# A two-layer hybrid encoder step on one core: an earlier rotary table, a longer sleep in the bf16 row norms, and sample loads that wait for the previous batch's pages

## The chip, the cores and the metric

The kernel runs on one core of one Trainium2 chip. The metric is the device time of one execution in microseconds, lower is better. Its instructions run on five engines: TensorE (PE, matmuls and transposes), VectorE (DVE), ScalarE (ACT), GpSimd (POOL) and SyncE (SP, which here issues most DMAs). Each engine works through its own queue in order.

## The reference, cut to what matters

Two layers run over the same 1168 columns: 16 meta tokens, 1024 prompt frames and 8 sample streams of 16 frames each. A layer has three parallel groups of heads (latent attention, mLSTM, gated DeltaNet), whose gated outputs are mixed back into the stream:

```python
proj = rms_norm(x, norm_w) @ w_in
(c_q, c_kv, k_r, z_a, m_q, m_k, m_v, m_i, m_f, m_o, z_m, g_qkv, g_a, g_b, z_g) = split(proj)
q = rms_norm(c_q, q_norm) @ w_uq          # 8 heads, 64 plain and 32 rotary columns each
q_rope = apply_rope(q[..., 64:], pos)
c_new = rms_norm(c_kv, kv_norm)           # the latent rows, 256 wide
o_a = mla_attention(...)                  # prompt: plain; samples: absorbed, over 1056 cached latent rows each
...
mixed = concat([o_a * silu(z_a), o_m * silu(z_m), o_g * silu(z_g)])
x = x + mixed @ w_out
```

For the samples, the attention of each of the 8 batches reads its own cached latent rows (1040 x 256) twice: transposed for the scores, and by rows for the product of probabilities and rows.

## The kernel before, in words

The order of the instructions is made while the kernel is built, by a small planner (`Weave`). It keeps a clock `W.t` that each matmul (`mm`) and transpose (`tr`) advances by a cost written into the code, and a list of threads (generators). A thread that yields a number sleeps that many microseconds of the planner's clock; one that yields a key waits until the key is in `D1`. While no thread is due, the planner takes the next piece of the filler `main()`: in each layer the projections `projs` (24 matmuls for each output tile and slice of columns, with split weights so that fp32r and bf16 products together give fp32), then the attention projections `qkv`, `out_first` and `out_proj`. So a sleep is a number of PE matmuls of the filler that are put between two pieces of a thread. The framework then orders the other engines' queues by the same dependences.

Large tiles are pages: 28 (`NPG`) of 128 x 1200 floats. `pg()` takes one, `free()` gives it back, and `room(n)` says whether n are left. A thread that needs pages asks `room` and sleeps for a number of its own until it is answered with yes.

The change touches three places.

`rstd` (L480 to L517) makes the scale of a row norm: column sums of squares by matmuls against a column of ones, then on DVE and POOL the power -0.5 (L495, L496), a split of the result into two parts (L499, L500), diagonals with the scale on them (L506, L508), a sleep, and two matmuls of those diagonals against a matrix of ones (`onesr`) that broadcast the scale. With `b16` the column sums take bf16 parts. `prep` is the only caller with `b16`: two norms (the latent rows `ckv`, the query latents `cq`) in each of three column slices, in each layer.

`prep` (L1347 to L1382) then scales and splits the latents, stores the new latent rows, transposes the sample columns of them (L1375), copies and stores these to `tok` and frees `ckv`. `qkv` (L1387 on) starts when `prep` is done and 10 pages are free. It takes two pages for the rotary table `tabq`, loads them, and multiplies the rotary query tiles (j = 0 and 3) by them (L1420, L1423, added on POOL at L1425). The rotary rows go to `qS` in HBM and come back to be split (L1530, L1531); between them lie the k and v projections (L1458 to L1483).

The samples run as six threads over 8 batches. `samp_load` takes three pages of raw rows for a batch (two of `latT`, one of `krT`), as long as fewer than 5 (`RP`) are in flight and 5 pages (1 + `SR`) are free; it asks every 0.3 us. `samp_split` splits them (L1698 to L1702), `samp_s` makes the scores and exponentials (L1753). `samp_ln` takes two pages for the rows `latN` of a batch, when 4 pages (2 + `SP`) are free; it asks every 8.8 us and, from batch 2 on, waits first for the end (`su`) of the batch two before. `samp_t` transposes the probabilities and multiplies them with `latN`; its last copies are at L1796.

Of the kernel before, what the change touches and what calls it, by code (L numbers as in the profile page):

```python
# [19 lines left out]
T = 1168  # L20
# [8 lines left out]
SR = 4  # L29
SP = 2  # L30
RP = 5
# [276 lines left out]
def _build(nc, tc, ctx, I, O, layers):  # L308
# [13 lines left out]
    def nm(p):  # L322
        uid[0] += 1
        return f"{p}{uid[0]}"

    def pg(dt=F32):
        n = nm("pg")
        t = pgp.tile([128, 2 * PG if dt == BF16 else PG], dt, tag="pg", name=n)
        pages[id(t)] = t
        if len(pages) > NPG:  # L330
            raise RuntimeError("out of pages")
        return t

    def free(*ts):
        for t in ts:
            del pages[id(t)]

    def room(n):
        return len(pages) + n <= NPG

    def need(n):
        while not room(n):
            yield 0.09
# [7 lines left out]
    def pb():  # L351
        return pbp.tile([128, 512], F32, tag="pb", name=nm("pb"))
# [4 lines left out]
    def wt(tag, w=128, bufs=2, dt=F32):  # L357
        return wk.tile([128, w], dt, tag=tag, name=nm("wk"), bufs=bufs)

    def mm(out, lhsT, rhs, start, stop):  # L360
        W.last = P.matmul(out, lhsT, rhs, start=start, stop=stop)  # L361
        n = rhs.free_size()
        if rhs.dtype == BF16:
            W.t += max(n / 2.4, 35.0)
        elif rhs.dtype != F32:
            W.t += max(n / 2.4, 107.0)
        else:
            m = lhsT.free_size()
            W.t += max(n / 0.6, 216.0) if m > 64 else max(n / 0.6, 124.0) if m > 32 else 85.0 if lhsT.partition_size() > 32 else 40.0
# [8 lines left out]
    def gate(inst):  # L378
        if W.last is not None:
            tc.add_manual_dep(inst.ins, W.last.ins.name, NOSYNC, reason="order of slots")  # L380

    def ld(dst, src, eng=None):
        gate((eng or nc.sync).dma_start(dst, src))

    def st(dst, src):
        nc.sync.dma_start(dst, src)
# [34 lines left out]
    def negh(w):  # L421
        return neg1.to_broadcast([128, w])
# [4 lines left out]
    def vcol(l, n, j):  # L427
        o = (l * VW + VEC[n][0]) if l < L else 2 * VW
        return vec[:, o + j:o + j + 1]
# [35 lines left out]
    def sumsq(pgs, w, s0, s1):  # L465
        acc = wt("hp", 528, 3)
        for k, p_ in enumerate(pgs):
            if k == 0:
                S.activation(acc[:, :w], p_[:, s0:s1], AF.Square)
            else:  # L470
                b = wt("th", 400)
                S.activation(b[:, :w], p_[:, s0:s1], AF.Square)
                V.tensor_add(acc[:, :w], acc[:, :w], b[:, :w])
        return acc[:, :w]

    def rstd(out, a, dim, s0, s1, b16=False):
        w = s1 - s0
        tl = [c for c in range(NT) if s0 <= OFF[c] < s1]
        ps = pb()
        col = wt("col", 8)  # L480
        V.memset(col, 1.0)
        if b16:
            ab = wt("th", 800, 2, BF16)
            ah, al = ab[:, :w], ab[:, 400:400 + w]
            S.copy(ah, a)
            V.tensor_sub(al, a, ah)
        for j, c in enumerate(tl):
            n, o = LEN[c], OFF[c] - s0
            if b16:
                mm(ps[:n, j:j + 1], ah[:, o:o + n], onesb, True, False)  # L490
                mm(ps[:n, j:j + 1], al[:, o:o + n], onesb, False, True)
            else:
                mm(ps[:n, j:j + 1], a[:, o:o + n], ones[:, 0:1], True, True)
        for j0, j1, n in (((0, 1, 16), (1, len(tl), 128)) if tl[0] == 0 else ((0, len(tl), 128),)):
            V.tensor_scalar(col[:n, j0:j1], ps[:n, j0:j1], 1.0 / dim, EPS, op0=ALU.mult, op1=ALU.add)  # L495
        G.tensor_tensor(col[:, 0:len(tl)], col[:, 0:len(tl)], negh(len(tl)), op=ALU.pow)  # L496
        nt = len(tl)
        ch = wt("ch", 8, 2, F32R)
        V.tensor_copy(ch[:, 0:nt], col[:, 0:nt])  # L499
        V.tensor_sub(col[:, 0:nt], col[:, 0:nt], ch[:, 0:nt].bitcast(F32))  # L500
        dg = wt("dg", 1024, 1, F32R)
        first = 16 if tl[0] == 0 else 0
        for e, c_ in enumerate((ch, col)):
            o = 512 * e
            if first:
                V.tensor_scalar_mul(dg[:, o:o + 16], ident[:, 0:16], c_.bitcast(F32)[:, 0:1])  # L506
            m = nt - (first > 0)
            V.tensor_tensor(dg[:, o + first:o + w].rearrange("p (j t) -> p j t", t=128),  # L508
                            ident.unsqueeze(1).to_broadcast([128, m, 128]),
                            c_.bitcast(F32)[:, nt - m:nt].unsqueeze(2).to_broadcast([128, m, 128]), op=ALU.mult)  # L510
        yield 2.70
        ps = pb()
        for e in range(2):
            mm(ps[:, :w], onesr, dg[:, 512 * e:512 * e + w], e == 0, e == 1)
        if out is None:
            return ps[:, :w]
        S.copy(out, ps[:, :w])  # L517

    def norm_split(p_, rp, wcol, hi, lo, s0, s1):
        V.scalar_tensor_tensor(p_[:, s0:s1], p_[:, s0:s1], wcol, rp, op0=ALU.mult, op1=ALU.mult)  # L520
        split(p_[:, s0:s1], hi[:, s0:s1], lo[:, s0:s1])
# [65 lines left out]
    def layer(l, XH, XLp, XL, xres, xw, R):  # L587
# [3 lines left out]
        D1 = W.done = {}  # L591
# [751 lines left out]
        def prep():  # L1343
            yield ("cq", 2)
            yield from need(2)
            cq = [D1["cq", j] for j in range(3)]
            ckv = [D1["ckv", j] for j in range(2)]  # L1347
            r1, r2 = pg(), pg()
            for s0, s1 in SLICES:
                w = s1 - s0  # L1350
                yield from rstd(r1[:, s0:s1], sumsq(ckv, w, s0, s1), 256.0, s0, s1, True)
                yield from rstd(r2[:, s0:s1], sumsq(cq, w, s0, s1), 384.0, s0, s1, True)
            while not room(4):
                yield 3.47
            yield 5.44
            hl = {}
            for n_, p_, r_, v_ in (("ck", ckv, r1, "kvn"), ("cq", cq, r2, "qn")):
                hl[n_] = []
                for k, t_ in enumerate(p_):
                    yield from need(2)  # L1360
                    hi, lo = pg(F32R), pg(F32R)
                    for s0, s1 in SLICES:
                        norm_split(t_, r_[:, s0:s1], vcol(l, v_, k), hi, lo, s0, s1)
                        yield 6.23
                    hl[n_].append((hi, lo))
                    if n_ == "cq":
                        free(t_)
                free(r_)
                if n_ == "ck":
                    for k in range(2):  # L1370
                        st(O["oLat"][l, k], ckv[k][:, :T])
                        G.tensor_copy(new[:, 128 * k:128 * k + 128], ckv[k][:, TP:T])
                    ps = pb()
                    for k in range(2):
                        tr(ps[:, 128 * k:128 * k + 128], ckv[k][:, TP:T], ident)  # L1375
                    t_ = wt("hp", 528, 3)
                    S.copy(t_[:, 0:256], ps[:, 0:256])
                    st(tokS, t_[:, 0:256])
                    free(*ckv)
                A.update({n_ + "h": [x_[0] for x_ in hl[n_]], n_ + "l": [x_[1] for x_ in hl[n_]]})  # L1380
            D1["prep"] = 1

        KS = ((0, 348), (348, 694), (694, 1040))

        def qkv():
            while "prep" not in D1 or not room(10):
                yield "idle"  # L1387
            tab, qs = [pg(), pg()], pg()
            A["qs"] = qs
            for j in range(2):  # L1390
                ld(tab[j][:, :T], I["tabq"][j])
            ckh, ckl, cqh, cql = A["ckh"], A["ckl"], A["cqh"], A["cql"]

            def load(t_):
# [272 lines left out]
        def samp_load():  # L1667
            yield "sprep"
            fly = A["fly"] = []
            for b in range(8):  # L1670
                for k in range(3):
                    while len(fly) >= RP or not room(1 + SR):
                        yield 0.30
                    raw = pg()
                    fly.append(raw)
                    p_, src = (slice(0, 128), I["latT"][l, b, :, k]) if k < 2 else (slice(0, 96), I["krT"][l, b])
                    ld(raw[p_, :TP], src)
                    G.tensor_copy(raw[p_, TP:NK], new[p_, 128 * k + 16 * b:128 * k + 16 * b + 16])
                    D1["raw", b, k] = raw, W.t / 1000.0 + YL
                    yield 0.00  # L1680
# [290 lines left out]
        A = {}  # L1971
# [20 lines left out]
```

## Time and profile before

| | |
|---|---|
| median of 3 runs | 2650.75 us (2647.45 to 2651.11) |
| the profiled execution | 2646.51 us, its span 2644.6 us |
| mean granted clock of PE | 0.978 |
| PE busy | 2488.7 us (94%) |
| PE weight loads | 2150.1 us (81%) |
| DVE, ACT, POOL busy | 58%, 42%, 29% |
| DMA | 97 GB/s over the span |

The profile is of one execution. A row of its timeline gives the start and length of an instruction, its engine and source line, what it writes and reads, and in brackets how long the engine stood idle before it and what ended that (idle time followed by "<-" and the instruction or DMA that came last). The granted clock is the share of full speed that PE was given in a stretch.

### The profile page before, as it was taken

The page shows a single profiled execution, that of the slowest core. Times are in us where ns is not written, and L with a number is a line of the kernel's source. Part 1 is how long each engine was busy: PE and PEld are TensorE (multiplying, and loading weights), DVE is VectorE, ACT ScalarE, POOL GpSimd, SP SyncE. Part 2 cuts the span into 40 slices and gives each one's busy share as a digit, 9 for nine tenths or more (in the row PEclk, how much of TensorE's full clock was granted, in tenths as well). Part 3 has the DMA queues.
Part 4 walks back from the last instruction along what each step waited for, and adds up shares of the span by engine and source line. Part 5 has one row for each costly group of instructions (what it writes and reads, how often), then busy time and mean ns, then how long its engine had stood idle before and what let it go on. Part 6 is the DMA issues. An engine that isn't in the chain of part 4 may idle for free. (4 is left out here: it accounts for less than half of the span.)

```text
span 2644.6 us, 45521 instructions
## 1 busy us (share of the span) xinstructions
PE 2488.7 (94%) x17310; PEld 2150.1 (81%) x17310; DVE 1530.2 (58%) x3716; ACT 1116.4 (42%) x2635; POOL 764.6 (29%) x865
## 2 busy tenths in 40 slices
PE   6999999999999899979998999999999999999997
PEld 4887888878878789779977888788788788897896
DVE  6667475464453476654566774755743526665636
ACT  5363444444433433442343544444444434334612
POOL 3122222122123543232441222221221245332414
PEclk9999999999999999989998999999999999998998
DMA  3212112121123644464422121221211245444832
GB/s 130 73 39 70 51 53 83 51 69 51 59 71 126 179 119 123 126 219 163 141 76 51 43 75 52 62 73 51 69 52 58 85 157 149 113 121 147 286 117 80
DMA packets 158411, 258.67 MB, mean 98 GB/s; under 512 B 48704, under 2 KB 110768, under 8 KB 158192
## 3 DMA queue, kind: packets, MB, share of 16 engines
q1 hardware_dynamic: 152224, 247.59, 30.0%
q0 software_dynamic: 1856, 3.86, 0.7%
q10 hardware_dynamic: 4112, 4.30, 0.7%
q8 instruction: 137, 2.24, 0.3%
q14 instruction: 82, 0.67, 0.1%
HBM read 190.77 MB, written 64.92 MB: 97 GB/s over the span
## 5 line engine op out<-in xcount | busy, mean ns | idle before, releaser
L361 PE MATMUL pa<-pg,wh 128*128 128x384 f32 (+3 forms) x6324 | 1317.8, 351 | 17.7 <-DVE pg L441 7.0
L361 PEld LDWEIGHTS pa<-pg,wh 128*128 128x128 f32 x6324 | 1104.6, 190 | 59.9 <-issue 8.5
L361 PE MATMUL pb<-pg,pg 128*128 128x352 f32 (+26 forms) x1908 | 425.1, 338 | 18.3 <-DVE sm L1553 4.4
L361 PE MATMUL pa<-pg,wb 128*128 128x384 bf16 (+1 forms) x2208 | 420.3, 330 | 4.7 <-POOL pg L544 3.6
L361 PEld LDWEIGHTS pb<-pg,pg 128*128 128x128 f32 (+7 forms) x1908 | 301.1, 188 | 70.8 <-issue 14.0
L361 PEld LDWEIGHTS <-wb 128*128 128x128 bf16 x2208 | 201.6, 98 | 141.6 <-issue 28.9
L361 PE MATMUL pb<-wk,pg 128*128 128x128 f32 (+4 forms) x2168 | 223.1, 250 | 20.2 <-ACT wk L983 5.2
L441 POOL TENSOR_TENSOR wh<-wf,wh 128x1024 fp32r<-128x1024 f32 (+1 forms) x61 | 144.4, 2367 | 323.1 <-ACT wh L437 316.7
L361 PEld LDWEIGHTS pb<-wk,pg 128*128 128x128 f32 (+3 forms) x2168 | 194.2, 161 | 41.9 <-issue 16.7
L1590 ACT ACTIVATE wk<-pb 128x320 f32<-128x320 f32 (+8 forms) x288 | 114.1, 407 | 241.9 <-PE pb L361 222.5
L361 PE MATMUL pa<-wk,pg 128*128 128x320 f32 (+8 forms) x576 | 190.9, 417 | 1.9 <-ACT wk L1590 1.3
L437 ACT CAST wh<-wf 128x1024 fp32r<-128x1024 f32 (+1 forms) x122 | 126.4, 1036 | 129.8 <-PE pa L361 119.5
L1553 DVE TENSOR_REDUCE sm<-pb 128x1 f32<-128x348 f32 (+9 forms) x232 | 107.9, 493 | 102.4 <-PE pb L361 89.9
L1613 DVE RECIPROCAL wk<-pa 64x320 f32<-64x320 f32 (+2 forms) x48 | 110.7, 2305 | 48.2 <-PE pa L361 47.5
L361 PE MATMUL pb<-wk,wk 32*32 32x16 f32 (+6 forms) x1776 | 110.6, 216 | 13.7 <-DVE wk L1131 4.5
L1531 POOL TENSOR_TENSOR pg<-pg,pg 64x520 fp32r<-64x520 f32 (+1 forms) x64 | 86.9, 1369 | 111.0 <-ACT pg L1530 87.9
L868 DVE SCALAR_TENSOR_TENSOR pg<-pg,vec,pg 128x1192 f32<-128x1192 f32 x72 | 107.1, 1503 | 18.4 <-ACT pg L866 18.1
L441 DVE TENSOR_TENSOR wh<-wf,wh 128x1024 fp32r<-128x1024 f32 (+1 forms) x61 | 78.6, 1289 | 53.5 <-ACT wh L437 53.4
L693 ACT COPY pg<-pa 128x384 f32<-128x384 f32 (+1 forms) x108 | 52.1, 482 | 134.6 <-PE pa L361 133.4
L457 ACT CAST wb<-wf 128x1024 bf16<-128x1024 f32 x92 | 96.2, 1045 | 26.6 <-PE pa L361 20.1
L361 PEld LDWEIGHTS pa<-wk,pg 128*128 128x128 f32 (+1 forms) x576 | 97.9, 193 | 5.9 <-ACT wk L1590 1.9
L361 PEld LDWEIGHTS pb<-wk,wk 32*32 32x32 f32 (+2 forms) x1776 | 73.1, 122 | 32.3 <-issue 9.3
(298 smaller groups left out, 3205.7 us busy)
## 6 DMA issues: line engine op xcount, KB each, us to landing
wf<-win SPq DMA_DIRECT2D x92, 512.0 KB
pg<-latT SPq DMA_DIRECT2D x32, 520.0 KB
pg<-latN SPq DMA_DIRECT2D x32, 512.0 KB
wf<-wout SPq DMA_DIRECT2D x24, 512.0 KB
xa<-wk SPq DMA_DIRECT2D x40, 192.0 KB
mix<-pg SPq DMA_DIRECT2D x12, 584.0 KB
pg<-mix SPq DMA_DIRECT2D x12, 584.0 KB
mix<-pg SPq DMA_DIRECT2D x12, 576.0 KB
```

The source lines that it names most:

```text
L361: W.last = P.matmul(out, lhsT, rhs, start=start, stop=stop)
L437: S.copy(hi, src)
L441: lo_eng.tensor_sub(lo, src, hi.bitcast(F32))
L457: S.copy(wb[:, :n], wf)
L693: S.copy(o[:, s0:s1], ps)
L868: V.scalar_tensor_tensor(y[:, :n], cb[:, j:j + n], vcol(l, "cw", 4 * ti + j), y[:, :n], op0=ALU.mult, op1=ALU.add)
L1531: G.tensor_sub(lo, raw, hi.bitcast(F32))
L1553: V.tensor_reduce(mx[:LEN[c], 3 * c + i_:3 * c + i_ + 1], ps[:LEN[c], :n1 - x_], axis=AX.X, op=ALU.min)
L1590: S.activation(pt[:m, :b - a], ps, AF.Exp, scale=-1.0)
L1613: V.reciprocal(rc, po[d, :w])
```

## The change

One sleep in `rstd` becomes longer where the row norm has bf16 parts. The two pages and loads of the rotary table move from the start of `qkv` into `prep`, right behind the store of the transposed sample columns and the freeing of `ckv`; `qkv` takes them over and asks for 8 free pages instead of 10. And `samp_load` doesn't take a page for batch b > 0 before `samp_ln` has taken batch b-1's.

```diff
--- before.py
+++ after.py
@@ -508,7 +508,7 @@
-        yield 2.70
+        yield 4.00 if b16 else 2.70
         ps = pb()
@@ -1377,18 +1377,19 @@
                     S.copy(t_[:, 0:256], ps[:, 0:256])
                     st(tokS, t_[:, 0:256])
                     free(*ckv)
+                    A["tab"] = [pg(), pg()]
+                    for j in range(2):
+                        ld(A["tab"][j][:, :T], I["tabq"][j])
...
         def qkv():
-            while "prep" not in D1 or not room(10):
+            while "prep" not in D1 or not room(8):
                 yield "idle"
-            tab, qs = [pg(), pg()], pg()
+            tab, qs = A["tab"], pg()
             A["qs"] = qs
-            for j in range(2):
-                ld(tab[j][:, :T], I["tabq"][j])
             ckh, ckl, cqh, cql = A["ckh"], A["ckl"], A["cqh"], A["cql"]
@@ -1669,7 +1670,7 @@
                 for k in range(3):
-                    while len(fly) >= RP or not room(1 + SR):
+                    while len(fly) >= RP or not room(1 + SR) or b and ("ln", b - 1) not in D1:
                         yield 0.30
                     raw = pg()
```

## Rows read from the trace of the kernel before

**Rows 1.** The page's busy times: engine, us, share of the span, instructions.
```profile
PE 2488.7 (94%) x17310; PEld 2150.1 (81%) x17310; DVE 1530.2 (58%) x3716; ACT 1116.4 (42%) x2635; POOL 764.6 (29%) x865
```

**Rows 2.** PE's waits, 750:790, then 2060:2096: us in total, times, longest.
```profile
PE pb L361 <- DVE wk L508: 5.1, 6, 2.3
...
PE pb L361 <- DVE wk L508: 4.2, 5, 1.5
```

**Rows 3.** Timeline of the first row norm: start, length, engine, line, operation.
```profile
753.15 2.39 POOL L441 TENSOR_TENSOR wh<-wf,wh 128x1024 fp32r<-128x1024 f32 x1
753.22 2.34 DVE L499 CAST wk<-wk 128x4 fp32r<-128x4 f32 x1 [1.13 <-POOL wk L496]
...
756.51 0.42 PE L361 MATMUL pb<-wk,onesr 128*128 128x400 f32 x1 [1.29 <-DVE wk L508]
```

**Rows 4.** Timeline of SP's queue around the table loads of layer 0.
```profile
830.10 0.33 SPq L386 DMA_DIRECT2D tok<-wk  x1
830.48 0.70 SPq L383 DMA_DIRECT2D pg<-tabq  x1
841.30 0.32 SPq L386 DMA_DIRECT2D mix<-pg  x1
841.73 0.37 SPq L383 DMA_DIRECT2D pg<-tabq  x1
```

**Rows 5.** Timelines of DVE, POOL, ACT and PE behind the table, layer 1 last.
```profile
845.45 0.57 DVE L1420 SCALAR_TENSOR_TENSOR pg<-pa,pg 128x400 f32<-128x400 f32 x1 [3.09 <-PE pa L361]
847.10 1.16 DVE L1423 SCALAR_TENSOR_TENSOR wk<-pa,pg 64x400 f32<-64x400 f32 x2 [1.08 <-DMA pg<-tabq]
...
851.04 2.40 POOL L441 TENSOR_TENSOR wh<-wf,wh 128x1024 fp32r<-128x1024 f32 x1
853.39 1.01 POOL L1425 TENSOR_TENSOR pg<-pg,wk 128x384 f32<-128x384 f32 x1
...
864.75 0.62 ACT L1530 CAST pg<-pg 96x520 fp32r<-96x520 f32 x1 [5.37 <-DMA pg<-qS]
...
865.77 6.46 PE L361 MATMUL pa<-wh,pg 128*128 128x512 f32 x21 [3.60 <-ACT pg L1459]
...
2173.78 6.55 PE L361 MATMUL pa<-wh,pg 128*128 128x512 f32 x16 [4.45 <-ACT pg L1459]
```

**Rows 6.** SP's queue in the sample stage: two rows of layer 0, one of layer 1.
```profile
1091.83 0.89 SPq L383 DMA_DIRECT2D pg<-latT  x2
...
1142.14 0.89 SPq L383 DMA_DIRECT2D pg<-latN  x2
...
2432.94 1.05 SPq L383 DMA_DIRECT2D pg<-latN  x2
```

**Rows 7.** PE's waits in 1130:1172, then in 2430:2475: us in total, times, longest.
```profile
PE pa L372 <- ACT pg L1753: 7.2, 3, 4.1
PE pb L361 <- DMA pg<-latN: 4.1, 1, 4.1
...
PE pb L361 <- ACT pg L1753: 2.3, 1, 2.3
```

**Rows 8.** Windows: us, busy (instructions) of PE, PEld, DVE, ACT, POOL, clock, DMA.
```profile
1130.00:1170.00 40.00, 26.13 (x150) 23.78 (x149) 22.21 (x35) 14.13 (x36) 14.97 (x24) 0.74 0.64 203
...
2435.00:2455.00 20.00, 16.69 (x101) 15.17 (x101) 15.09 (x26) 12.40 (x30) 11.47 (x18) 0.91 0.83 266
```

**Rows 9.** The last copies of the 8 batches, layer 0 and 1: ns, first and last.
```profile
L1796 DVE COPY pg<-pb x8: 291/292/293, 1153.4 to 1227.4; 128x128 f32<-128x128 f32 x8
...
L1796 DVE COPY pg<-pb x8: 291/292/294, 2457.0 to 2525.9; 128x128 f32<-128x128 f32 x8
```

**Rows 10.** A piece of the chain that ended last: start, us, what.
```profile
2442.64 3.68 DMA pg<-latT
```

**Rows 11.** Casts and subtractions of the sample splits, 1100:1230: ns min/median/max.
```profile
L1699 POOL TENSOR_TENSOR pg<-pg,pg x16: 1289/1318/1790, 1108.7 to 1198.1; 128x528 fp32r<-128x528 f32 x16
...
L1698 ACT CAST pg<-pg x32: 625/637/653, 1105.4 to 1196.5; 128x528 fp32r<-128x528 f32 x32
```

## The prediction

> **What bounds the kernel now.** I read the page's busy times first, then the waits and the timeline of TensorE (PE), then the windows of the stages that the change touches. PE is busy for 2488.7 of 2644.6 us of span [rows 1], so only two things can move the end: time in which PE does nothing (155.9 us in all), and time in which it works at the lower clock. Each part of the change is therefore priced by the PE waits beside it. The waits of the other engines count only where PE inherits them.
>
> The profiled run took 2646.51 us, 2644.6 of it span and 1.9 around it; the median of the runs shown is 2650.75, or 4.2 more. I make the sum against 2646.51 and put it onto the median at the end. A difference under 0.2% (5.3 us) is one that measuring this kernel can't tell from none.
>
> **Part 1: the sleep in the row norms, 2.70 to 4.00.** Only `prep` passes bf16, so this is 6 calls in each layer, 12 in all. After the sleep PE multiplies the scaled diagonals by ones to broadcast the scale, and it needs what DVE writes at L508. Today it waits for that 6 times in layer 0 (5.1 us, longest 2.3) and 5 times in layer 1 (4.2 us, longest 1.5) [rows 2]. The timeline shows why the size varies: in the first call the DVE cast of four columns took 2.34 us, beside a POOL subtraction of 2.39 us that began 0.07 us earlier, and the broadcast came 1.29 us late [rows 3]. The 1.3 us that the planner now sleeps longer is filled with projection matmuls that have to be done anyway. Of each wait at most 1.3 us goes: 2.3 leaves 1.0, 1.5 leaves 0.2, and those near 1.3 leave at most 0.1 or so. So 9.3 - 1.3 = 8.0 us is the most that 1.3 us of work can hide; I take 7.5, as PE's work in the planner's 1.3 us isn't exactly 1.3 us. Bounds: -9.3 (all waits gone) and -4 (the collisions return at the larger calls).
>
> The Trainium skill ("Perfetto Trace Analysis", Optimizing Scalar/DVE Operations) says that GpSimd and DVE share an SBUF read port that a two-port DVE instruction holds exclusively. By that rule a later broadcast doesn't shorten the cast, and waits return when another pair falls together; the 2.34 us row agrees with the rule. That result is a rival below, priced from rows.
>
> The cost: `prep` runs six times 1.3 = 7.8 us later in each layer. Its cover is the last gated projections (za, zg, zm), which PE works on until shortly before the last mix store at 841.30. The transposes of the new latent rows, whose store to `tok` is issued at 830.10 [rows 4], move to about 837.5, still ahead of that end. The attention projections can't start before those gated ones are through, now or then. So I cost the delay itself at nothing; without the cover it would be up to 7.8 us in each layer. What is late next is the table, part 2.
>
> **Part 2: the two table loads, moved into `prep`.** Today SP's queue holds tok store, table 0, mix store, table 1 [rows 4]. The mix store waits for the last gated projection, so table 1 is issued 11.25 us after table 0, at 841.73, and DVE's rotary multiply at L1423 then waits 1.08 us for it until 847.10 [rows 5]. The changed order puts both loads right behind the transposes; each is 128 x 1168 floats (584 KB) and is issued in 0.4 to 0.7 us. Both pass the mix store if they enter SP's queue before it, at about 838.5, some 3 us sooner for table 1 and 8 us later for table 0. By the 5.4 us between the issue and the use of table 1 today they land at about 844, and table 0 is first needed at 845.45. So the 1.08 us goes, with only some 1.5 us to spare.
>
> What is behind that wait: POOL's last rotary add (853.39, behind a 2.40 us weight split), the q stores and the load back, ACT's cast at 864.75 after 5.37 us of waiting, and PE, which waits 3.60 us at 865.77; layer 1 shows 4.45 at 2173.78 [rows 5]. This chain ends the wait of PE, so it hands on what it gains, and no more than its own wait: 1.0 us in each layer, -2 in all. If POOL's add also goes ahead of the weight split it is up to 3 each, -6. If the tables stay behind the mix store, both are issued from 841.7 on and table 0 is late by 1 to 2 us in each layer, +4. The pages cost nothing: two are taken sooner, the same two, and the stage now asks for 8 instead of 10.
>
> **Part 3: sample loads held.** The raw rows of batch b (three loads) are now not taken before batch b-1 has its pages of latent rows (`samp_ln`, room for 4, asked every 8.8 us; the raw loads ask every 0.3 us for room for 5). In layer 0 the raw loads win this race today: the first raw load is issued at 1091.83, but the latent rows of batch 0 only at 1142.14 [rows 6]. PE waits 7.2 us for ACT's exponentials and 4.1 us for those rows [rows 7]. From 1130 to 1170 it is busy 26.13 of 40 us at a granted clock of 0.74 [rows 8], between its levels of 1.2 and 2.4 GHz. In layer 1 the latent rows go out at 2432.94, while attention ends, PE waits 2.3 us [rows 6, 7], and 2435 to 2455 has 16.69 busy of 20 at 0.91 [rows 8]. The last batch ends 74.0 us after the first in layer 0, 68.9 in layer 1 [rows 9].
>
> So layer 0 has 13.9 us of idle time and layer 1 3.3. To this comes the clock: at most 26.13 x 0.26 = 6.8 us in layer 0, of which I take 4.5, since the low clock lies partly over idle time, and in layer 1 16.69 x 0.09 = 1.5. Layer 0 holds 18.4, layer 1 4.8.
>
> With the hold batch 0 gets its latent pages first, in both layers, and its scores and products can run in the tail of attention. What is late next: batch 2's raw rows, held until batch 1 has latent pages, which come free near the end of attention. From then a raw load takes 3.7 us to land [rows 10], its three loads 1.3 us to issue (0.89 us for two, [rows 6]), and the splits 5.1 us (six casts on ACT of about 0.64 us, then the last subtraction on POOL of 1.3 us, [rows 11]): about 10 us. PE has one batch of work against it, 68.9 / 7 = 9.8 us [rows 9], of which I take half as begun already. That leaves a hole of some 5 us in each layer, and 3 us more for the clock: about 8. Layer 0 goes from 18.4 to 8.5 (-10), layer 1 from 4.8 to 8 (+3). Part 3 is -7. Bounds: -17 (both holes nearly gone) and +5 (layer 0 gains 3, layer 1 loses 8). Behind the held loads on SP's queue stand only the later batches' own loads, since the planner holds them and not the queue. Afterwards batch b's raw rows have two batches' work of cover, 17 to 20 us against 10, so the steady pace stays PE's.
>
> The sum: 7.5 + 2 + 7 = 16.5 us less, 2630 against 2646.5; with the 4.2 us to the median that is 2634.2, given as **2635**.
>
> **The rivals.**
>
> Hold empties the pipeline (slower). Raw rows of batches 1 to 3 are no longer ahead when attention ends; layer 1, which has them today, falls to layer 0's state: 13.9 - 3.3 = 10.6 us of idle time and 6.8 - 1.5 = 5.3 of clock at most, some +15, while layer 0 keeps its hole. With 9.5 from parts 1 and 2 that is +5.5: 2656. It decides itself where load and split (10 us) are longer than PE's ready work at the end of attention, so if a poll of 8.8 us is missed. For it: the 8.8 us poll; against it: layer 0's hole is itself made of missing latent pages. The Trainium skill ("Trainium Kernel Development and Optimization", Best Practices) asks to overlap DMA with compute by double buffering, and a hold speaks against that; in layer 0 the trace doesn't agree, as up to five raw pages are in flight (RP) and PE waited for the other load [rows 7]. Chance 0.10.
>
> The hold nets nothing: layer 1 loses what layer 0 gains. Parts 1 and 2 stay, -9.5: 2641. For it: the two layers' estimates are of like size and opposite sign. Chance 0.25.
>
> Nothing moves much: part 1 gives 4, as collisions of DVE and POOL follow the later slots, table 0 is late (+2), part 3 is 0 to -2: 2647. For it: the late broadcasts are those with 2.34 us casts. Against it: the mean of the 11 waits is 0.85 us, well under the 1.3 us added, and only one is over 1.5. Chance 0.14.
>
> The hole closes in both layers: 7.5 + 2 + 17 = 26.5: 2624. For it: layer 1 shows a start with 3.3 us idle. Chance 0.14.
>
> The forecast, 2635, has the remaining 0.37.
>
> **How the numbers follow.** Cases below 2645.4 are the forecast, the closed hole, and most of the netted hold (0.23): 0.74. Within 0.2%: the rest of that and most of nothing moves, 0.15. Above 2656: 0.11, from the slower rival and tables behind the mix store. For 8 in 10 the range reaches from the lower part of the closed hole, 2618, to just under the slower rival, 2655; the forecast's own range is 2628 to 2641.
>
> **What would show it.** Part 1: the waits of PE for L508 fall from 9.3 to about 1.5 us, each broadcast about 1.3 us later behind its column matmuls. Part 2: both tables next to each other on SP ahead of the mix store, no wait at L1423, the wait before the v matmuls at 865.77 and 2173.78 shorter by 0.5 (the chain 1.0 sooner, PE too by 0.5 at the k matmuls). Part 3: layer 0's first latent rows issued well before attention ends, the wait for them gone, and one wait of some 5 us in each layer at batch 1 or 2. The prediction is wrong if layer 1's 2435 to 2455 gets over 8 us of idle time, if the latent rows of layer 0 still come after 1140, or if PE waits before the q matmuls at 845.

## The result, and the profile after

The changed kernel takes 2691.35 us (median of 4 runs, 2689.88 to 2691.61) where the one before takes 2649.1 (4 runs): the ratio is 1.0158, with a 95% interval of 1.014 to 1.0176, or 41.9 us slower. The prediction was 2635, and its range ended at 2655. The profiled execution has a span of 2688.1 us at a mean granted clock of 0.973, against 2644.6 and 0.978.

The first view is the page's busy times. PE has the same 17310 instructions as in [rows 1] and is busy for 26.5 us more, and 17 us of the growth of the span are more waiting:

```profile
PE 2515.2 (94%) x17310; PEld 2163.0 (80%) x17310; DVE 1525.0 (57%) x3716; ACT 1114.8 (41%) x2635; POOL 762.7 (28%) x865
```

Where the time came from is read from the starts of the same instruction in both traces (lines of after are one higher behind the inserted loads). The stretch ahead of the first norm has the same work in all the kernels here, and its end still differs by up to 4 us between profiles, so only steps from one mark to the next count. These too are good to a few us only: the kernel below that holds a batch in layer 0 alone does the same as before between layer 1's first q tile and its first sample cast, and its profile is 3.4 us shorter there.

| mark | before | after | later by | step |
|---|---|---|---|---|
| layer 0: first norm multiply in `prep` (DVE, L520) | 758.03 | 760.11 | 2.1 | |
| layer 0: first plain q tile off PSUM (ACT, L1427) | 840.66 | 850.29 | 9.6 | +7.5 |
| layer 0: first score reduction (DVE, L1553) | 879.70 | 892.21 | 12.5 | +2.9 |
| layer 0: last sample batch (DVE, L1796) | 1227.41 | 1244.70 | 17.3 | +4.8 |
| layer 1: first norm multiply in `prep` (DVE, L520) | 2067.67 | 2085.41 | 17.7 | +0.5 |
| layer 1: first plain q tile (ACT, L1427) | 2147.87 | 2173.14 | 25.3 | +7.5 |
| layer 1: last sample batch (DVE, L1796) | 2525.91 | 2569.16 | 43.2 | +18.0 |

So there are two places, each in both layers: the way from the norms into the attention projections, and the sample stage.

**Into the attention projections.** PE's waits in 740 to 900 are no longer those of [rows 2]; besides 0.7 us for L485, two releasers are new, the casts and subtractions of the query latents (ACT L437, DVE L441). Columns: us in total, times, longest.

```profile
PE pa L361 <- ACT pg L1460: 4.1, 2, 3.6
PE pb L361 <- DVE wk L508: 3.8, 4, 1.8
PE pa L361 <- DVE pg L441: 2.7, 2, 1.5
PE pa L361 <- ACT pg L437: 2.0, 1, 2.0
```

The timeline of 840 to 850 shows them at work: the transposes of the latent rows, the copy of these, and only then (behind one weight cast, left out here) all nine casts of the query latents in one burst, with PE waiting three times behind it.

```profile
840.80 0.38 PE L372 MATMUL pb<-cst,pg 128*128 128x128 f32 x2
841.38 0.37 ACT L1377 COPY wk<-pb 128x256 f32<-128x256 f32 x1
...
842.58 3.86 ACT L437 CAST pg<-pg 128x400 fp32r<-128x400 f32 x9
843.17 0.97 PE L361 MATMUL pa<-pg,wh 128*128 128x400 f32 x2 [1.99 <-ACT pg L437]
845.64 2.69 PE L361 MATMUL pa<-pg,wh 128*128 128x400 f32 x7 [1.50 <-DVE pg L441]
```

A third wait of this kind, 1.22 us, ends at 849.55. The window of 840 to 850 (us, busy of PE, PEld, DVE, ACT, POOL, granted clock, DMA share and GB/s) shows what it cost: nearly half of it idle, and a mean granted clock of 0.66, which lies between the two levels of 1.2 and 2.4 GHz; in the next 10 us it is 0.82.

```profile
840.00:850.00 10.00, 5.28 (x18) 3.86 (x17) 7.79 (x7) 5.44 (x12) 6.45 (x5) 0.66 0.52 185
```

And the tables didn't go out together. SP's queue, to be read against [rows 4]; the line left out is the mix store, at 843.24:

```profile
831.33 0.42 SPq L383 DMA_DIRECT2D pg<-tabq  x1
...
843.66 0.38 SPq L386 DMA_DIRECT2D tok<-wk  x1
844.09 0.89 SPq L383 DMA_DIRECT2D pg<-tabq  x1
```

**The sample stage.** The copies that end a batch (ns, first and last of the 8; layer 0, then layer 1) span 105.4 and 110.0 us, where [rows 9] have 74.0 and 68.9:

```profile
L1797 DVE COPY pg<-pb x8: 290/291/292, 1139.3 to 1244.7; 128x128 f32<-128x128 f32 x8
...
L1797 DVE COPY pg<-pb x8: 290/291/292, 2459.2 to 2569.2; 128x128 f32<-128x128 f32 x8
```

The hold did what it says: batch 0 ends at 1139.3 instead of 1153.4, though everything ahead of it is 12.5 us later. But the next four batches take 12.6 to 21.6 us each in layer 0 (the last three come with the output projection's matmuls between them, before and after). PE's waits of 1120 to 1250 have no large one any more; they are many small ones, for the casts (L1699) and subtractions (L1700) of the raw rows:

```profile
PE pb L361 <- ACT pg L1699: 4.5, 4, 1.2
PE pb L361 <- POOL pg L1700: 4.2, 6, 1.1
PE pb L361 <- DVE pg L1700: 3.4, 3, 1.3
```

One turn, layer 0, from the timeline of 1170 to 1203 (rows left out in between):

```profile
1170.96 0.89 SPq L383 DMA_DIRECT2D pg<-latT  x2
1185.36 0.80 SPq L383 DMA_DIRECT2D pg<-latT  x2
1188.88 0.29 DVE L1797 COPY pg<-pb 128x128 f32<-128x128 f32 x1 [2.59 <-PE pb L361]
1189.20 0.27 ACT L1797 COPY pg<-pb 128x128 f32<-128x128 f32 x1 [4.61 <-DVE pg L1797]
1189.37 2.23 ACT L1699 CAST pg<-pg 128x528 fp32r<-128x528 f32 x4
1190.05 2.27 PE L361 MATMUL pb<-pg,pg 128*128 128x352 f32 x9 [1.21 <-ACT pg L1699]
1192.03 0.55 ACT L1754 ACTIVATE pg<-pb,wk 128x352 f32<-128x352 f32 x1
1202.84 0.29 DVE L1797 COPY pg<-pb 128x128 f32<-128x128 f32 x1 [2.59 <-PE pb L361]
```

The raw rows of the 8 batches are issued in order and cast in order, so the rows can be counted off (batches 0 to 7). The casts at 1189.37 are those of batch 5, whose raw rows went out at 1170.96, 18.4 us before; the raw rows issued at 1185.36 are those of batch 6, cast at 1203.32. For batches 4 to 7 it is 13.5 to 18.4 us from issue to cast in the two layers, and no load ends a wait of ACT's from 1139 to 1245, so these casts don't wait for their load. They stand in ACT's queue right behind ACT's share of the copy that ends batch 3 (1189.20), and this waits for PE's products. Behind the casts come the scores of batch 5 on PE, which wait 1.21 us for them, and on ACT the exponentials of batch 4 (1192.03), without which the products of batch 4 can't run. These end at 1202.84, and the turn has taken 13.96 us. The kernel before has another order in ACT's queue, here in layer 1:

```profile
2478.25 0.27 ACT L1796 COPY pg<-pb 128x128 f32<-128x128 f32 x1 [2.44 <-DVE pg L1796]
2478.41 0.56 ACT L1753 ACTIVATE pg<-pb,wk 128x352 f32<-128x352 f32 x1
...
2480.01 1.18 ACT L1698 CAST pg<-pg 128x528 fp32r<-128x528 f32 x2
```

Behind the copy that ends batch 3 come at once the exponentials of batch 4, and only then casts. These are those of batch 6: they run one batch further ahead, while PE works on the products of batch 4. From 2460 to 2487 PE is busy there for 26.81 of 27 us at the full clock; in the changed kernel it is busy for 21.81 of the 28 us from 2500 to 2528, at a mean granted clock of 0.94.

### The profile page after: what moved, and what is told of

It is laid out like the page before. It is cut to its first block, busy times and chain, and to the rows that moved or that the text cites. A ratio compares the mean times of both kernels' runs of the same rounds, so it can differ in the third digit from the quotient of the medians.

```text
span 2688.1 us, 45486 instructions
## 1 busy us (share of the span) xinstructions
PE 2515.2 (94%) x17310; PEld 2163.0 (80%) x17310; DVE 1525.0 (57%) x3716; ACT 1114.8 (41%) x2635; POOL 762.7 (28%) x865
## 5 line engine op out<-in xcount | busy, mean ns | idle before, releaser
L361 PE MATMUL pb<-pg,pg 128*128 128x352 f32 (+26 forms) x1908 | 443.5, 345 | 41.8 <-ACT pg L1699 9.0
L361 PEld LDWEIGHTS pb<-pg,pg 128*128 128x128 f32 (+7 forms) x1908 | 308.0, 193 | 102.9 <-issue 14.2
L441 POOL TENSOR_TENSOR wh<-wf,wh 128x1024 fp32r<-128x1024 f32 (+1 forms) x63 | 149.1, 2367 | 332.1 <-ACT wh L437 325.8
L437 ACT CAST wh<-wf 128x1024 fp32r<-128x1024 f32 (+1 forms) x122 | 126.5, 1037 | 131.1 <-PE pa L361 120.9
L441 DVE TENSOR_TENSOR wh<-wf,wh 128x1024 fp32r<-128x1024 f32 (+1 forms) x59 | 74.7, 1267 | 71.9 <-ACT wh L437 71.6
L681 POOL TENSOR_TENSOR pg<-pg,wk 128x384 f32<-128x384 f32 (+1 forms) x48 | 49.1, 1024 | 185.9 <-DVE wk L463 176.4
```

Of the source, the lines that this page charges most:

```text
L437: S.copy(hi, src)
L441: lo_eng.tensor_sub(lo, src, hi.bitcast(F32))
L681: G.tensor_mul(o[:, s0:s1], o[:, s0:s1], th[:, :s1 - s0])
```

## The experiments

The runs of a group share their runs of before. Times in us are the ratio of the two kernels' runs, put onto the median of before of that group (2649.5, 2649.1 and 2651.2).

### The sleep alone

```diff
-        yield 2.70
+        yield 4.00 if b16 else 2.70
```

> The longer sleep alone, 4.00 instead of 2.70 in the bf16 row norms. Theory 1 (the sleep moves PE's work ahead of the broadcast, but the chain of DVE and POOL behind it moves too): PE's waits for L508 fall by 1 us at most in each layer, as the changed kernel shows 3.8 and 4.5 us where the one before had 5.1 and 4.2; the time stays within 4 us of before, 2646 to 2653. Theory 2 (the prediction's): 7.5 us less, 2641 to 2643. Theory 3 (the sleep alone pushes the transposes and splits of prep into the start of the attention projections): 5 to 15 us more.

Measured: 0.998 (0.9967 to 0.9992), or 5.3 us less (2.1 to 8.7). By the ratio that is 2644.2, between the windows of theories 1 and 2, and by the medians 2646.2, just inside that of theory 1; the interval takes in parts of both, and theory 3 falls. The waits decide against the prediction's theory. PE's waits in 740 to 900:

```profile
PE pb L361 <- DVE wk L508: 3.9, 4, 1.8
PE pa L361 <- ACT pg L1459: 2.3, 2, 2.1
PE pb L361 <- ACT wk L485: 0.8, 1, 0.8
```

Those in front of the broadcasts fell from 5.1 to 3.9, and 0.8 came back at L485, in front of the column sums. In layer 1 they were 4.2 and are 3.7 and 0.8. The timeline of the second norm shows why, broadcast, column sums and broadcast in turn:

```profile
760.76 0.96 PE L361 MATMUL pb<-wk,onesr 128*128 128x400 f32 x2
765.05 0.40 PE L361 MATMUL pb<-onesb,wk 128*16 128x1 bf16 x7
767.95 0.42 PE L361 MATMUL pb<-wk,onesr 128*128 128x400 f32 x1 [0.82 <-DVE wk L508]
```

In the kernel before, these column sums followed the first broadcast at once. Now they end at 765.45, 3.7 us after it, and PE gets to the second broadcast 1.7 us after them (3.0 before); the longer sleep went partly in front of the column sums. The last broadcast of the layer still waits 1.85 us. So of 8.0 us that 1.3 us of work could hide, the waits gave back 0.1 net (9.3 before; 3.9 + 0.8 + 3.7 + 0.8 = 9.2). The steps between marks agree: from the first norm multiply to the first q tile layer 0 is 0.2 us longer and layer 1 0.4. The rest of the 5.3 us lies further on, in the wait before the v matmuls (3.6 and 4.5 before, 2.3 in each layer now) and in the sample stage of layer 0 (3.4 less from the first sample cast to the last batch), where the planner's later clock moved other pieces. Which of these moves carries it wasn't tried.

### The table alone

```diff
                     free(*ckv)
+                    A["tab"] = [pg(), pg()]
+                    for j in range(2):
+                        ld(A["tab"][j][:, :T], I["tabq"][j])
...
-            while "prep" not in D1 or not room(10):
+            while "prep" not in D1 or not room(8):
```

> The earlier table alone, with the sleep of 2.70. Theory 1 (pages are handed out in program order, so the table's pages, whose loads come behind the latent transposes, hold up the pages of the query latents' splits; without the longer sleep the transposes come at about 830 and the splits, 8 us of ACT, DVE and POOL, end near 839): from 2 us less to 4 us more, PE waits under 2 us at the start of the attention projections. Rival (the table costs the same with or without the sleep): 14 to 18 us more over the two layers, with waits of some 4.7 us for the casts and subtractions of the splits.

Measured: 0.9991 (0.9979 to 1.0004), 2.4 us less, which isn't told from none. Theory 1 holds: PE's only waits in 740 to 900 are 5.1 us for L508 and 3.8 us before the v matmuls, and the one for L1423 is gone. The rival, 14 to 18 more, falls. ACT's rows of 825 to 850 show that the casts of the query latents do stand behind the transposes, as theory 1 has it, and end at 836.3, still ahead of the attention projections at 839.5:

```profile
829.76 0.37 ACT L1377 COPY wk<-pb 128x256 f32<-128x256 f32 x1 [2.91 <-PE pb L372]
831.25 3.03 ACT L437 CAST pg<-pg 128x400 fp32r<-128x400 f32 x7
835.37 0.91 ACT L437 CAST pg<-pg 128x384 fp32r<-128x384 f32 x2
```

### Sleep and table together

Both diffs above.

> Sleep and table together, without the hold. Theory 1 (the two interact: the sleep moves the transposes to 841, the table's pages come behind them, and the splits behind these start only there): 13 to 19 us more, with 4 to 5 us of PE waits at the start of the attention projections of each layer and the lower clock after them, though each of the two alone costs under 4. Rival (additive): the sum of the two single runs.

Measured: 1.0049 (1.0034 to 1.0065), 13.0 us more. The sum of the two alone would be 7.7 us less, so together they make 20.7 us that neither makes alone, and the additive rival falls. PE's waits in 740 to 900 have the new ones of the changed kernel, 3.0 and 2.0 us, among them:

```profile
PE pa L361 <- DVE pg L441: 3.0, 2, 1.8
PE pa L361 <- ACT pg L437: 2.0, 1, 2.0
```

Its ACT row is that of the changed kernel too: nine casts in one burst, behind the transposes.

```profile
839.88 0.37 ACT L1377 COPY wk<-pb 128x256 f32<-128x256 f32 x1
...
841.08 3.86 ACT L437 CAST pg<-pg 128x400 fp32r<-128x400 f32 x9
```

### The table's loads not tied to PE

`ld` ties a load, in the order that the framework makes, to the last PE instruction that the planner had placed, here the transposes of the latent rows. This kernel is the last one with plain DMAs in the place of `ld`.

```diff
-                        ld(A["tab"][j][:, :T], I["tabq"][j])
+                        nc.sync.dma_start(A["tab"][j][:, :T], I["tabq"][j])
```

> Sleep and table together as in e4, without the hold, but the table's loads are plain DMAs that aren't tied to the last PE instruction, so they can take their pages and go out before the transposes. Theory 1 (the 13 us of e4 come from the tie: pages are given in program order, the tied load holds the table's pages open until the transposes at 841, and the splits' pages stand behind them): the splits run before 835 again, the waits for their casts and subtractions at the attention projections (5.0 us in layer 0) are gone, and the time is that of the two single runs together, 2640 to 2645. Rival (the two pages taken sooner are what is missing, whoever waits for what): 2657 to 2667, with the waits as in e4. Second rival (the loads go out sooner and collide with the other transfers): the splits early, but 2646 to 2655.

Measured: 0.9995 (0.9983 to 1.0006), 1.3 us less. Theory 1's mechanism holds, and the rival (the pages as such) falls: the pages are taken at the same point of the program, and the 13 us are gone. SP sends both tables at 804.87, and ACT casts the query latents from about 808 (the first row still has three casts of the latent rows) to 822.6, far ahead of the transposes' copy at 840.16:

```profile
804.87 0.94 SPq L1382 DMA_DIRECT2D pg<-tabq  x2
...
806.96 2.60 ACT L437 CAST pg<-pg 128x400 fp32r<-128x400 f32 x6
...
821.22 1.36 ACT L437 CAST pg<-pg 128x400 fp32r<-128x400 f32 x3 [1.65 <-POOL pg L441]
...
840.16 0.37 ACT L1377 COPY wk<-pb 128x256 f32<-128x256 f32 x1
```

The time of the two alone together, 7.7 us less, wasn't reached: 2647.8 by the ratio lies in the window of the second rival, a collision of the earlier loads with other transfers, which nothing here tests. The intervals of this run (4.5 less to 1.6 more) and of the sleep alone (8.7 to 2.1 less) overlap, so that isn't told apart. What the trace shows is a wait of 4.0 us before the v matmuls in layer 0 and 3.3 in layer 1, where the sleep alone has 2.3 in each.

### The hold alone

```diff
-                    while len(fly) >= RP or not room(1 + SR):
+                    while len(fly) >= RP or not room(1 + SR) or b and ("ln", b - 1) not in D1:
```

> The hold of the sample loads alone. Theory 1 (the hold makes every batch's raw load wait for pages that come free two batches before, so each of the 8 batches runs at the pace of load and split, 12.6 to 14 us, instead of 8.4 to 8.8): 22 to 29 us more, of it about 20 in layer 1 and 5 in layer 0. Rival (the prediction's, only one hole for each layer): 3 to 10 us less. Second rival (the stage is slow because the shifted start of attention changed its polls, not by the hold): within 5 us of before.

Measured: 1.009 (1.0076 to 1.0104), 23.8 us more; both rivals fall. From the first sample cast to the last batch layer 0 is 5.1 us longer and layer 1 18.7. Batch 0 ends early in both layers, and the last batch ends 106 us after it in each:

```profile
L1796 DVE COPY pg<-pb x8: 291/292/293, 1130.9 to 1236.6; 128x128 f32<-128x128 f32 x8
...
L1796 DVE COPY pg<-pb x8: 290/292/293, 2450.0 to 2556.3; 128x128 f32<-128x128 f32 x8
```

With the 13.0 of sleep and table this makes 36.8 of the 41.9 us; the difference of 5.1 is about what the three intervals leave open.

### The hold with a poll of 0.3 us

```diff
-                    yield 8.80
+                    yield 0.30
```

> The hold as in e3, and the thread that takes the latent pages asks every 0.3 us instead of every 8.8. Theory 1 (the pace is set by pages that come free two batches before, then load and split; the question is asked once and answered at once): within 6 us of e3, 2669 to 2682. Rival (the 8.8 us poll misses the free pages and holds everything behind it, as the prediction's slower case had it): back to 2645 to 2660.

Measured: 1.0077 (1.0064 to 1.009), 20.4 us more. The poll, on which the prediction's slower rival turned, carries about 3 of 24 us, and the intervals of the two runs (20.1 to 27.6 more and 17.0 to 23.8 more) don't tell that from nothing.

### The hold for batches 2 to 7 alone

```diff
-                    while len(fly) >= RP or not room(1 + SR):
+                    while len(fly) >= RP or not room(1 + SR) or b > 1 and ("ln", b - 1) not in D1:
```

> The hold for batches 2 to 7 alone, batch 1 free. Theory 1 (the cost is the steady order: the scores free pages, the latent rows take them, the raw rows come last and their load and split stand before the next scores): at least the 20 us of the full hold, 2669 to 2685, 12 to 14 us for each later batch, and layer 0 without the early start. Rival (the order of the first two batches sets the pace of all): within 6 us of before, 2643 to 2655.

Measured: 1.0102 (1.0085 to 1.0118), 27.0 us more. The cost is in the steady order and not in the start: from the third batch's end on they are again 12.6 to 14.0 us apart in layer 0, until the output projection comes in, as these rows show. One part of the expectation missed: layer 0's early start is there without the hold of batch 1 (batch 0 ends at 1134.29, in the kernel before at 1153.40).

```profile
1167.23 0.29 DVE L1796 COPY pg<-pb 128x128 f32<-128x128 f32 x1 [3.42 <-PE pb L361]
1181.20 0.29 DVE L1796 COPY pg<-pb 128x128 f32<-128x128 f32 x1 [2.59 <-PE pb L361]
1193.77 0.29 DVE L1796 COPY pg<-pb 128x128 f32<-128x128 f32 x1 [2.59 <-PE pb L361]
```

### The hold loosened by one batch

```diff
-                    while len(fly) >= RP or not room(1 + SR):
+                    while len(fly) >= RP or not room(1 + SR) or b > 1 and ("ln", b - 2) not in D1:
```

> The hold loosened by one batch: raw rows of batch b wait for the latent pages of batch b-2. Theory 1 (with b-1 the raw rows wait for the end of batch b-3 and have one batch's work ahead of them, with b-2 they wait for the end of b-4 and have two): the pace is 8.4 to 8.8 us again and the time within 8 us below or 3 above before, 2641 to 2653. Rival (any hold makes the load wait for pages, and the raw loads lose their turn to the latent ones): 2660 to 2675.

Measured: 0.9999 (0.999 to 1.0007), 0.3 us less. One batch of freedom takes the whole cost away. In ACT's queue the casts of batches 4 to 7 again stand behind the exponentials and ahead of the copies of the batch two before; in the changed kernel and in the three with the unloosened hold (alone, with the short poll, for batches 2 to 7) the casts of batches 3 to 6 stand right behind these copies. And from issue to cast of the raw rows it is only 8.9 to 11.7 us here (batches 4 to 7), less than the changed kernel's 13.5 to 18.4, with 8.2 to 9.0 us for a batch in layer 1: the time between load and cast isn't what the hold costs. Layer 0's stage is 7 us shorter from the first sample cast to the last batch (7.3 us late at its start, 0.3 at its end), and layer 1's about 3 to 5 longer.

### The hold for batch 1 alone

```diff
-                    while len(fly) >= RP or not room(1 + SR):
+                    while len(fly) >= RP or not room(1 + SR) or b == 1 and ("ln", 0) not in D1:
```

> The hold for batch 1 alone (its raw rows wait for batch 0's latent pages, later batches are free as before). Theory 1 (the cost of the hold is its steady state, and its use is only at the start, where layer 0 lost the race for pages): 3 to 12 us less than before, mostly in layer 0; batches 2 to 7 again 8.4 to 8.8 us apart. Rival (the cost is at the start, where the hold delays the first loads): 8 us or more above before. Second rival (the hold of one batch changes nothing, as the pages are short for later batches as well): within 3 us of before.

Measured: 1.0006 (0.9992 to 1.002), no change, which the expectation gave to the second rival. But the marks show two changes that cancel: from the first sample cast to the last batch layer 0 is 6.9 us shorter and layer 1 7.5 longer.

### The hold for batch 1 of layer 0 alone, and with the sleep

```diff
-                    while len(fly) >= RP or not room(1 + SR):
+                    while len(fly) >= RP or not room(1 + SR) or l == 0 and b == 1 and ("ln", 0) not in D1:
```

> The hold for batch 1 of layer 0 alone. Theory 1 (holding the first batch takes 7 us out of layer 0's sample stage and, in layer 1, where the latent pages came in time already, puts 3 to 8 us in, so that both layers together showed no change): 4 to 8 us less than before, 2641 to 2645, and layer 1 as before. Rival (the gain seen in layer 0's stage is given back later, by the output projection that has fewer filler pieces left): within 2 us of before.

Measured: 0.9989 (0.9976 to 1.0001), 2.9 us less by the ratio (medians 2646.9 and 2651.15), short of the 4 to 8 expected and not told from none. In its trace layer 0's stage is 7.2 us shorter and layer 1's unchanged (6.4 less at its first sample cast, 6.3 at its last batch).

With the sleep of 4.00 in addition:

> The sleep of 4.00 and the hold for batch 1 of layer 0. Theory 1 (the two lie in stages that don't touch): the sum of e1 (3 to 5 us less) and e9 (4 to 8 less), so 7 to 13 us less than before, 2636 to 2642. Rival (the shifted plan of the attention stage changes who wins the race for pages): within 5 us of before.

Measured: 0.9963 (0.995 to 0.9975), 9.8 us less than before, 2638.45: faster than both kernels. The first latent rows go out at 1117.53, where [rows 6] have 1142.14, and the wait of 4.1 us for them [rows 7] is gone. Its batches 2 to 4 end 8.2 to 8.8 us apart:

```profile
1159.29 0.29 DVE L1796 COPY pg<-pb 128x128 f32<-128x128 f32 x1 [6.47 <-PE pb L361]
1167.48 0.28 DVE L1796 COPY pg<-pb 128x128 f32<-128x128 f32 x1
1176.23 0.29 DVE L1796 COPY pg<-pb 128x128 f32<-128x128 f32 x1
1184.94 0.29 DVE L1796 COPY pg<-pb 128x128 f32<-128x128 f32 x1
```

The two largest of PE's waits in 1110 to 1175 are 2.8 and 2.3 us, both for exponentials (L1753). The sum of the sleep alone and this hold alone would be 8.2 us less, so the two add up, as theory 1 has it.

### Those two, and the table's loads not tied to PE

> The sleep, the table loads that aren't tied to PE's last instruction, and the hold for batch 1 of layer 0. Theory 1 (three places that don't touch, the table's own 1 us in each layer on top): at or up to 3 us under e10, 2634 to 2642. Rival (as in e5, where sleep and untied table gave less than the sleep alone: the earlier tables bring nothing, since the wait before the v matmuls stays): 1 to 5 us above e10.

Measured: 0.9966 (0.9954 to 0.9978), 9.0 us less. The untied table brings nothing measurable on top; the intervals of this kernel and the last one nearly coincide, so neither of the two expectations is told from the other.

## Why the prediction was wrong, point by point

**Part 1, the sleep: the size held by chance, the reason didn't.** The forecast was 7.5 us less from waits at L508; alone the sleep gives 5.3 less, within the bounds of 4 to 9.3. But the waits in front of the broadcasts and column sums went from 9.3 only to 9.2. The step "of each wait at most 1.3 us goes" assumed that the whole added work lies between column sums and broadcast. Some of it lies in front of the next column sums, which wait on a copy of their own (L485). Nor are the late broadcasts those with the 2.34 us casts, as the rival on part 1 has it: the longest wait of before, 2.32 us at 783.84, stands behind a cast of 0.99 us (780.73).

**Part 1's cost at nothing: right for the sleep alone, not beside part 2.** The transposes did move, to 840.8 instead of 837.5, and still end ahead of the gated projections, as said. Alone that was free. What the step didn't follow is who stands behind the transposes once part 2 is there.

**Part 2, "the pages cost nothing": this is the step that failed first.** Alone, the table gives 2.4 us less where 2 were forecast, with the wait at L1423 gone. With the sleep it makes 20.7 us. The runs bear out this mechanism: the loads are tied to the transposes, the pages of the query latents' splits are asked for behind the table's pages, and so the splits run behind the transposes too: from 831 without the sleep (free), from 841 with it (13 us over both layers), from 808 with the tie taken away (free). That pages are handed out in program order is inferred from these three places of the splits; no row shows it directly. What the rows of ACT show is the order in its queue: the casts stand behind the copy of the transposes where the loads are tied, and ahead of it where they aren't. The loads' own time isn't it: in the changed kernel the first cast starts at 842.58, and the second table is only issued at 844.09, behind the mix store, with no wait at the table's multiplies (L1424). The range's upper end for the tables, 4 us, was worked out for the tables' own arrival alone.

**Part 3, the steady pace: the largest error.** The forecast was 7 less, with bounds of 17 less and 5 more; alone the hold costs 23.8. Its first half held: batch 0 starts early, layer 0's first wait goes, and a hold limited to that start shortens layer 0's stage by 7 us against 10 forecast. The step that failed is "batch b's raw rows have two batches' work of cover, 17 to 20 us against 10, so the steady pace stays PE's". The cover is there, 13.5 to 18.4 us from issue to cast; the pace isn't PE's all the same. The 10 us took load and split (casts and subtractions) together as something that runs beside PE, and didn't ask where the split comes in ACT's queue. With the hold it comes one batch later, behind the end of batch b-2, and the scores of batch b and the exponentials of batch b-1 come behind it. This turn of copy, casts, scores and exponentials, products takes 12.6 to 14.0 us for a batch at best, where PE needs 8.2 to 8.8, as the three batches of the fastest kernel show. Batches 2 to 7 alone show the whole cost, and one batch of freedom removes it, though it shortens the time from load to cast. That one batch fits the planner's keys: raw rows of batch b wait for the latent rows of b-1, and those for the end of b-3, with the looser hold of b-4. How the keys become the place in ACT's queue is argued from the code, and no row shows it. A lack of free pages isn't shown either: asking for them every 0.3 us left 20.4 of the 23.8 us. One smaller term was short too: the raw load of batch 1 in layer 1, issued behind two latent loads, landed after 9.28 us and ACT waited for it, where the sum had 3.7 [rows 10].

**The rivals.** The slower one had the right sign and part of the place, with a price of 15 us instead of 24, and its point of decision, the 8.8 us poll, is worth some 3 us that aren't told from none. The netted hold (layer 1 loses what layer 0 gains) came out nearly to the microsecond, but for the hold of batch 1 alone. No rival put two parts of the change together. The Trainium skill's line on overlapping DMA with compute ("Trainium Kernel Development and Optimization", Best Practices), which the prediction set aside since raw pages were already in flight, doesn't settle it: with the hold the raw loads still run under the work of other batches, 13.5 to 18.4 us ahead of their casts, and what it took away was the split of the next batch under the products of this one.

**What the prediction said would show it.** The first latent rows of layer 0 did move ahead of 1140 (to 1129.57), which it counted for itself; that sign was right while the time went the other way. PE's waits before the q matmuls, named as a sign of error, are there (1.99 and 1.50 us). The third sign, more than 8 us of idle time in layer 1's start, isn't: the time went into the batches behind it.

## What to carry to other kernels

When a hold or a tie decides who gets a buffer first, follow it through the steady state, and not only the start that looked bad: here the start gained 7 us in one layer, and the hold as a whole lost 24 over both. It isn't enough that a load is early: ask where the work on the loaded data then stands in the queue of each engine, and what stands behind it. A load that is moved takes its buffers with it, and what asks for buffers after it in the program can end up behind it; ask what it is tied to, and where that lands when another edit moves it. Two edits that are each free can share one cover, so the pair has to be priced as a pair.

## What the runs showed of the hardware

The cast of a few columns that took 2.34 us in [rows 3] is long, in every trace here, where a POOL instruction begins 0.05 to 0.08 us ahead of it, and it ends with that instruction, to within 0.04 us. In the changed kernel's timeline of 750 to 795 the first call has it again (2.34 us at 755.30, POOL's subtraction at 755.23), and the last call of the layer has it too:

```profile
788.58 2.36 POOL L441 TENSOR_TENSOR wh<-wf,wh 128x1024 fp32r<-128x1024 f32 x1
...
788.65 2.32 DVE L499 CAST wk<-wk 128x3 fp32r<-128x3 f32 x1 [0.96 <-POOL wk L496]
```

In the kernel before, that call's cast took 0.99 us (780.73), beside a shorter POOL subtraction; others take 0.17. So the longer sleep left the first call's long cast as it was and gave the last call one too, whose broadcast waits 1.84 us. Where POOL's instruction begins after the cast, the cast is short, as in this pair of the kernel with sleep and table:

```profile
13.13 0.17 DVE L499 CAST wk<-wk 128x4 fp32r<-128x4 f32 x1 [1.13 <-POOL wk L496]
13.19 2.35 POOL L441 TENSOR_TENSOR wh<-wf,wh 128x1024 fp32r<-128x1024 f32 x1
```

So in these pairs it is the cast that waits, for the POOL instruction that began first. The Trainium skill's rule that GpSimd and DVE share a read port that a two-port DVE instruction holds exclusively ("Perfetto Trace Analysis", Optimizing Scalar/DVE Operations) agrees in that the two don't run together; the holder here is POOL, and that it is the port is not shown. The prediction had the rule as a rival, with part 1 at 4 us less; the waits agree with the rival's mechanism, and the time, 5.3 us less (2.1 to 8.7), doesn't tell its 4 from the forecast's 7.5.
